# Score products of a head pair in one group per query tile, and a scheduler that counts changes of TensorE's array mode

## The chip, the cores and the metric

The program runs on one NeuronCore of a Trainium2 chip. The metric is device time in microseconds of one execution. The kernel before has a median of 554.98 us over three runs (554.88 to 555.44).

The core has five instruction streams that run beside each other and wait for each other through semaphores: TensorE (PE; its weight loads are listed apart as PEld), VectorE (DVE), ScalarE (ACT), GpSimd (POOL) and the DMA queue's engine (SP). Each takes its instructions in the order of the program.

## What is computed

One decoder layer over 1024 tokens of width 1024, in float32. `h` is the normalised input, scaled and shifted by a projection of the conditioning vector. One projection of `h` gives everything else:

```python
u_pool, g_pool, q, k, v, g_attn, qi, ki, wi = split(h @ w_in)
pool_out = pool_mixer(u_pool) * silu(g_pool)
# for each block of 128 queries:
score = sum_heads(relu(qi . ki) * wi)          # 8 index heads of 64, all 1024 keys
sel   = top_k(score, 256)                      # causal
p     = softmax(q . k[sel] / 8);  o = p @ v    # 8 heads of 64, 2 key heads
y     = concat(pool_out, o * silu(g_attn)) @ w_out
x     = x + gate * y
```

The selection is done by threshold: the kernel finds each query's 256th score by bisection over its bits, and adds a mask of zero or -1e30 to all scores in place of gathering keys.

## The kernel before, in words

Products are made from split operands: a float32 operand is cut into a rounded part and a rest (`hhi`, `hlo`; `wh`, `wl`), and three matmuls stand for one. Such a matmul is 128x128 by 128x512. The two kinds of score products (`ki` by `qi`, and `k` by `q`) are plain float32 with a contraction of 64. A pair of heads lies in the two halves of the 128 partitions, so the products of a pair use the upper and the lower 64 rows of the array. The products of probabilities with `v` are 64 columns wide, two side by side. So TensorE works in three array modes: all of the array, row halves, column halves. In the order of the program a float32 product is one instruction; in the trace it is two.

The text of the kernel does not fix the order of the work. It is written as generators ("strands"): each yields its next instruction (`Op`), a group of instructions that are to stand together (`Group`), a choice between engines (`Either`), a place in a pool (`Place`) or a condition. A planner, `Flow.run`, holds a clock for each engine with its own estimates of durations, and always issues the request with the least value of `wait`, to which it adds the strand's rank: `s[1]` (a number from `EARLY`, chosen by the kind under which the strand was spawned), or for a TensorE request `LAST` of that kind. So a change of the numbers `EARLY`, `LAST`, `SAFE`, `HOP` or `FAVOUR` moves instructions on all engines. `Op.wait` of a TensorE operation adds `safe`, which makes the planner issue it later than its data.

The parts that the prediction speaks of:

- `main_line`: the projection of `h` (`m<-hhi,wh` and its kind, fills TensorE from about 23 us to 329 us), in an order of tiles written in `ORDER`: `a` gates, `q` queries, `m` the pooling mixer (`u` and `gp`, then `mix`: `u` by a small matrix, `gp`, and its split `mph`, `mpl`).
- `index_scores`: for query tile 7 down to 2 and four head pairs, the products `m<-kiT,qix`; `score_relus` takes them out of PSUM on ACT (`kt`), and `score_sums` adds them up on DVE (`score`). PSUM has eight banks, and a place in it can be refused while fewer than `keep` are free (`IK`, `QK`).
- `selection`: the bisection, for tiles 5, 6, 7 on ACT (`ajunk`, then the small `aq`, `xq`), for tiles 2, 3, 4 on DVE (`junk`, `aq`, `xq`). 15 bits, then 16 bits. Between them and at the end DVE works on the masks (`selw`, `key`).
- `unit(i)`, i = 0 to 7: attention of a query tile. Products `m<-kT,qr`; `maxima` on DVE adds the mask and takes the maximum (`ex`, `mx`; it empties the bank); `exps` on ACT; `turns` transposes on TensorE (`m<-c,ex`), copied out as `pw`; `products` (`m<-pw,vrow`); `gated` (`mah`, `mal`). Unit i may start when unit i-1-FLY has ended.
- `output_line`: `project_pooled` (`m<-mph,wh`), then the first and the second half of `project_attended` (`m<-mah,wh`), 96 matmuls each for the halves. The second half needs all eight units and is the last work of the program.

Of the kernel before, what the change touches and what calls it, by code (L numbers as in the profile page):

```python
# [24 lines left out]
MASK_NEG = -1.0e30  # L25
KVW = 328

ORDER = "a2 a0 a1 q0 q1 | q2 m1 q3 m3 m2 m0 a3"
SWAP16 = [(i + 16) % 32 for i in range(32)]
WARM = [()] * 8  # L30
GROUPS = (((5, 6, 7), True), ((2, 3, 4), False))
# [4 lines left out]
ROOM = {"b": 36, "ld": 2, "st": 3, "wh": 4, "wl": 4, "kt": 2, "sg": 2, "selw": 1, "m": 8}  # L36


EARLY = {"main": 0.6, "fill": 0.4, "weights": 0.0, "evac": -1.0, "side": 0.2, "h": -0.2, "mods": -0.2, "select": -0.1,
         "scores": -0.6, "attend": -1.1, "late": 1.0, "kv": -0.3, "qi": -0.8, "pick": -0.6}  # L40

SELECT = -0.6
LAST = {"main": 0.12, "fill": 0.08}

SAFE = {"side": 1.0}

SCALED = (0,)

SUMS = (0,2,4,)

WKM = 6


HOP = 0.13
PHOP = 0
STT = 0.06
HOPS = {"PE": 0.19, "DVE": 0.13, ("ACT", "DVE"): 0.14, ("ACT", "ACT"): 0.035}

AGE = 0.37

PW_POOL = 0.4
XO_POOL = 0.38
BACK = 0.5
SPAN = 0.5

QK = 3
IK = 4
FK = 2
PK = 0
# [1 line left out]
MIX = 4  # L71
KEEP = 6

FLY = 1

PV = 2

WA_AHEAD = 3
AHEAD = 3
XN_AHEAD = 2  # L80

FAVOUR = {"DVE": 0.12, "ACT": -0.13, "POOL": 0.05}
TABLES = {AF.Silu: 1, AF.Sqrt: 2, AF.Exp: 3}


# [6 lines left out]
class Op:  # L92


    def __init__(self, eng, name, fn, args, kw):
        self.eng, self.name, self.fn, self.args, self.kw = eng, name, fn, args, kw
        aps = [a for a in args if isinstance(a, bass.AP)]
        named = [a for k, a in kw.items() if isinstance(a, bass.AP)]
        self.outs, self.ins = [], []
        for a in aps[:1] + [kw[k] for k in ("accum_out",) if kw.get(k) is not None]:  # L100
            self.outs.append(store(a))
            if a.free_size() == 1:
                self.outs.append((store(a), a.offset))
        for a in aps[1:] + named:
            self.ins.append((store(a), a.offset) if a.free_size() == 1 else store(a))
        self.us, self.safe = self._cost(aps, kw), 0.0
        self.shared = self._shared(aps)

# [12 lines left out]
    def _cost(self, aps, kw):  # L121
        size = [a.free_size() for a in aps]
        n = max(size)
        eng = self.eng
        if eng == "SP":
            return 0.42
        if eng == "PE":
            rate = 2 if self.name == "transpose" else 4 if aps[1].dtype == F32 else 1
            if rate == 4 and min(aps[0].shape[0], aps[1].shape[0]) == 64:
                rate = 2  # L130
            return max(0.109, size[0] * 0.000417 * rate + 0.0135)
        wide = [a for a, k in zip(aps, size) if k == n]
        psum = any(a.space == PSUM for a in wide)
        half = all(mybir.dt.size(a.dtype) == 2 for a in wide)
        if eng == "ACT":
            t = 0.000833 * n + (0.05 if psum else 0.094)
            t += 0.093 * sum(isinstance(kw.get(k), bass.AP) for k in ("scale", "bias", "accum_out"))
            return t
        if eng == "POOL":
            if self.name == "tensor_tensor":  # L140
                return 0.0021 * n + 0.147
            return 0.000833 * n + 0.16
# [28 lines left out]

    def issue(self, flow):
        t = self.start(flow)
        us = self.us
        if self.shared:
            flow.port = (t + us, self.eng)
        if self.eng == "ACT":
# [78 lines left out]
class Flow:  # L256
# [2 lines left out]

    def __init__(self):  # L260
        self.clock = dict.fromkeys(("PE", "DVE", "ACT", "POOL", "SP"), 0.0)
        self.dma, self.table = 0.0, None
        self.port, self.landed = (0.0, None), []
        self.ready, self.used, self.left, self.tag = {}, {}, {}, {}
        self.room = {k: [0.0] * n for k, n in ROOM.items()}
        self.strands = []
# [45 lines left out]
                req.issue(self)  # L312

    def spawn(self, gen, kind="side"):
        s = [gen, EARLY[kind], None, kind]
        self.strands.append(s)
        self.forward(s, None)

# [5 lines left out]
    def forward(self, s, val):  # L324
        try:
            s[2] = s[0].send(val)
            for o in s[2].ops if isinstance(s[2], Group) else [s[2]]:
                if isinstance(o, Op) and o.eng == "PE":
                    o.safe = SAFE.get(s[3], 0.0)
        except StopIteration:  # L330
            self.strands.remove(s)

# [28 lines left out]
def hybrid_layer(ctx, tc, xT, cT, nwT, badaT, wada, wq, wet, wkv, qnw, knw, wpool,  # L361
# [4 lines left out]
    flow = Flow()  # L366
# [526 lines left out]
    def index_scores():  # L893
        yield lambda: bool(ki)
        for i in (7, 6, 5, 4, 3, 2):
# [6 lines left out]
            for e in range(NH // 2):  # L902
                yield lambda: e in qi
                both = [], []
                for t, got in enumerate(both):
                    relus.append((i, 2 * e + t, got))
                for c0 in range(0, n, 512):
                    c1 = min(n, c0 + 512)
                    ops, put = [], []
                    for t in range(2):  # L910
                        ps = yield bank(keep=IK - 1 if t else IK)
                        r = slice(t * 64, t * 64 + 64)
                        ops.append(mm(ps[:, :c1 - c0], qi[e][r, i * P - 256:(i + 1) * P - 256],
                                      ki["T"][r, c0:c1], True, True))
                        put.append((c0, c1, ps))
                    yield Group(ops)
                    for t in range(2):
                        both[t].append(put[t])
        flow.drop(ki["T"], *[qi[e] for e in range(NH // 2)])

    parts = []
# [272 lines left out]
    def unit(i):  # L1194
# [42 lines left out]
        for e in range(4):  # L1237
            both = [], []
            for t in range(2):
# [2 lines left out]
                o = len(ex) % per * n  # L1242
                ex.append(slots[-1][:, o:o + n])
                flow.spawn(maxima(2 * e + t, both[t]), "attend")
            for c0 in range(0, n, 512):
                c1 = min(n, c0 + 512)
                ops, put = [], []
                for t in range(2):
                    ps = yield bank(keep=QK - 1 if t else QK)
# [3 lines left out]
                yield Group(ops)  # L1253
                for t in range(2):
                    both[t].append(put[t])
        if i == NT - 1:
            flow.drop(kT[0], *qT.values())

# [248 lines left out]
```

## Time and profile before

| | |
|---|---|
| median of the runs | 554.98 us |
| the profiled execution | 553.77 us |
| its span, first to last instruction | 552.1 us |
| PE busy | 516.8 us, 94% |
| DVE, ACT, POOL busy | 423.7, 372.5, 168.5 us |
| chain that ended last | PE 57%, DVE 27%, ACT 7%, issue 5% |

The profile shows one execution. A busy PE is not a PE at its best: its matmuls overlap, and how fast they follow each other is read from their starts in the timeline. PEclk is the granted clock as a share of 2.4 GHz. The stages overlap; by TensorE's work they are: start (to 103 us), index products between projections (103 to 172), projections while the selection runs (to 338), pooled output between attention units 0 to 4 (338 to 435), units 5 to 7 with the first half of the attended output (435 to 526), second half (to 552).

### The profile page before, as it was taken

What the parts mean: (1) busy time and instruction counts of PE and PEld (TensorE: products, weight loads), DVE (VectorE), ACT (ScalarE), POOL (GpSimd) and SP (SyncE); (2) the same over time, 40 slices, a digit from 0 to 9 for tenths busy, and PEclk for the clock granted to TensorE, in tenths of its full rate; (3) what the DMA queues carried; (4) which work ended last, traced back from release to release, by engine and by line L of the source; (5) the groups of instructions that cost most, each with busy time, mean ns of one, the idle gap of its engine ahead of it and who ended that gap; (6) DMA issues with size and microseconds to landing.
All of it is one profiled execution on the core that took longest, in us unless ns stands there. A gap on an engine that the chain in (4) does not pass through costs nothing.

```text
span 552.1 us, 7620 instructions
## 1 busy us (share of the span) xinstructions
PE 516.8 (94%) x2492; PEld 377.9 (68%) x2492; DVE 423.7 (77%) x895; ACT 372.5 (67%) x841; POOL 168.5 (31%) x179
## 2 busy tenths in 40 slices
PE   6969999999999999999997995999998999897997
PEld 6758899655657778868875863766676556545675
DVE  0699896787788999999999997985757996357142
ACT  6456721676478998998935988989896457818420
POOL 1399290221100246532434452420212242012000
PEclk9989999999999999999998997999999999998999
DMA  8994518010210111111110131634435222004044
GB/s 306 406 405 126 175 45 292 28 58 19 77 59 0 39 39 57 58 39 39 39 38 20 39 114 60 207 96 155 134 126 176 81 79 95 1 19 150 23 150 155
DMA packets 28023, 58.29 MB, mean 106 GB/s; under 512 B 3792, under 2 KB 7888, under 8 KB 27984
## 3 DMA queue, kind: packets, MB, share of 16 engines
q1 hardware_dynamic: 27984, 57.81, 30.5%
q8 instruction: 19, 0.31, 0.2%
q14 instruction: 20, 0.16, 0.1%
HBM read 47.32 MB, written 10.49 MB: 105 GB/s over the span
## 4 chain that ended last, share of the span: by engine, by line
PE 57%; DVE 27%; ACT 7%; issue 5%; DMA 2%; POOL 1%; SPq 0%; DVEq 0%; POOLq 0%; ACTq 0%
PE m L182 57%; DVE junk L182 9%; ACT ex L182 4%; DVE selw L182 3%; DVE ex L182 3%; DMA xt<-xT 2%; DVE sw L182 1%; DVE xq L182 1%; DVE mx L182 1%; ACT ajunk L182 1%; DVE wa L182 1%; DVE nx L182 1%; DVE aq L182 1%; DVE key L182 1%; DVE hlo L182 1%
## 5 line engine op out<-in xcount | busy, mean ns | idle before, releaser
L182 PE MATMUL m<-hhi,wh 128*128 128x512 f32 (+1 forms) x320 | 121.6, 402 | 1.0 <-ACT hhi L182 1.0
L182 PE MATMUL m<-hlo,wh 128*128 128x512 f32 (+1 forms) x320 | 115.2, 385 | 4.5 <-DVE hlo L182 4.5
L182 PE MATMUL m<-hhi,wl 128*128 128x512 f32 (+1 forms) x320 | 115.4, 382 | 0.0
L182 ACT ACTIVATE ajunk<-key,xq 128x768 bf16<-128x768 uint16 (+2 forms) x93 | 96.5, 1038 | 5.8 <-DVE xq L182 4.6
L182 PEld LDWEIGHTS m<-hhi,wh 128*128 128x128 f32 x320 | 59.5, 191 | 25.8 <-issue 12.4
L182 DVE TENSOR_SCALAR_CACHE_REDUCE junk<-key,xq 128x384 bf16<-128x384 uint16 (+2 forms) x93 | 69.3, 745 | 2.8
L182 PEld LDWEIGHTS m<-hlo,wh 128*128 128x128 f32 x320 | 59.2, 190 | 17.0 <-DVE hlo L182 5.3
L182 POOL TENSOR_TENSOR wl<-ld,wh 128x512 fp32r<-128x512 f32 x42 | 63.3, 1512 | 20.3 <-ACT wh L182 11.3
L182 ACT ACTIVATE ex<-ex,mx,c 128x256 f32<-128x256 f32 (+6 forms) x64 | 54.8, 858 | 19.4 <-DVE mx L182 13.3
L182 PEld LDWEIGHTS m<-hhi,wl 128*128 128x128 f32 x320 | 59.4, 190 | 12.3 <-issue 1.7
L182 POOL TENSOR_SCALAR wh<-ld 128x512 fp32r<-128x512 f32 x28 | 19.6, 698 | 108.3 <-PE m L182 96.1
L182 DVE SCALAR_TENSOR_TENSOR score<-kt,c,score 128x1024 f32<-128x1024 f32 (+5 forms) x42 | 42.9, 1022 | 11.3 <-ACT kt L182 9.4
L182 ACT ACTIVATE kt<-m 128x512 f32<-128x512 f32 (+1 forms) x80 | 37.9, 527 | 13.8 <-DVE score L182 8.6
L182 PE MATMUL m<-c,ex 128*128 128x128 f32 x288 | 37.8, 284 | 7.3 <-ACT ex L182 7.1
L182 PEld LDWEIGHTS m<-c,ex 128*128 128x128 f32 x288 | 33.8, 147 | 11.2 <-ACT ex L182 9.2
L182 PE MATMUL m<-kT,qr 64*128 64x512 f32 (+3 forms) x192 | 39.6, 511 | 1.6 <-DVE mx L182 1.6
L182 DVE SCALAR_TENSOR_TENSOR xo<-m,c,xo 128x512 f32<-128x512 f32 x24 | 17.9, 748 | 28.4 <-PE m L182 27.0
L182 DVE CUSTOM_DVE_ANT_0 ex<-m,key 128x512 f32<-128x512 f32 (+1 forms) x48 | 30.5, 663 | 7.8 <-PE m L182 7.8
L182 PE MATMUL m<-kiT,qix 64*128 64x512 f32 (+3 forms) x160 | 34.1, 542 | 0.0
L182 PEld LDWEIGHTS m<-kT,qr 64*128 64x128 f32 x192 | 18.7, 186 | 21.8 <-issue 13.7
L182 PE MATMUL m<-pw,vrow 128*64 128x512 f32 x144 | 33.3, 600 | 0.0
L182 PE MATMUL m<-mph,wh 128*128 128x512 f32 x64 | 26.4, 413 | 4.5 <-DVE mph L182 4.5
(186 smaller groups left out, 1017.4 us busy)
## 6 DMA issues: line engine op xcount, KB each, us to landing
wa<-wada SPq DMA_DIRECT2D x24, 512.0 KB, 7.5
ld<-wet SPq DMA_DIRECT2D x16, 512.0 KB, 3.3
ld<-wout SPq DMA_DIRECT2D x24, 256.0 KB, 2.9
xo<-xT SPq DMA_DIRECT2D x16, 256.0 KB, 3.2
y_d<-xo SPq DMA_DIRECT2D x16, 256.0 KB, 2.3
xo<-y_d SPq DMA_DIRECT2D x16, 256.0 KB, 2.9
outT<-xo SPq DMA_DIRECT2D x16, 256.0 KB, 2.1
xt<-xT SPq DMA_DIRECT2D x7, 512.0 KB, 7.7
```

The source lines that it names most:

```text
L182: self.fn(*self.args, **self.kw)
```

## The change

The products of a head pair are collected over all keys of the query tile and yielded as one `Group` (two or four products), for the index scores and for attention; before, each stretch of 512 keys was a group of two. The first place of a group is asked for with `keep` `IK` (`QK`), each further one with one less.

The planner knows array modes: an operation with a contraction of 64 is "rows", one with 64 output partitions "columns", any other "all"; when the mode changes, the planner's TensorE clock is moved by `SWITCH` of the mode that is left. Strands are ranked by the name of their generator where `EARLY` (and `SAFE`) has it, else by their kind as before. Many of the planner's numbers are others. Attention may run two units ahead (`FLY` 2), and two loads may start earlier (`WKM`, `WA_AHEAD`).

```diff
-ORDER = "a2 a0 a1 q0 q1 | q2 m1 q3 m3 m2 m0 a3"
+ORDER = "a2 a0 a1 q1 q2 | q0 m1 q3 m3 m2 m0 a3"
 EARLY: the old entries, and 24 new ones by generator, as
+         "mix": -0.36, "rotated": -0.18, "query_loads": 0.01, "exps": -0.11, "score_sums": -1.13,
-SELECT = -0.6
-LAST = {"main": 0.12, "fill": 0.08}
+SELECT = -0.461
+LAST = {"main": 0.12, "fill": 0.129, "scores": 0.008}
-SAFE = {"side": 1.0}
+SAFE = {"side": 1.0, "unit": 0.1, "query_norms": 0.67, "rotated": 0.7, "norm": 0.45, "weight_loads": 0.1}
-WKM = 6
+WKM = 4
+SWITCH = {"all": 0.1, "rows": 0.25, "columns": 0.32}
-QK = 3
+QK = 4
-FLY = 1
+FLY = 2
-WA_AHEAD = 3
+WA_AHEAD = 5
...
     def issue(self, flow):
         t = self.start(flow)
+        if self.eng == "PE" and self.mode != flow.mode:
+            t = max(t, flow.clock["PE"] + SWITCH[flow.mode])
...
     def spawn(self, gen, kind="side"):
-        s = [gen, EARLY[kind], None, kind]
+        s = [gen, EARLY.get(gen.__name__, EARLY[kind]), None, kind]
...
+                ops, put = [], []
                 for c0 in range(0, n, 512):
                     c1 = min(n, c0 + 512)
-                    ops, put = [], []
                     for t in range(2):
-                        ps = yield bank(keep=IK - 1 if t else IK)
+                        ps = yield bank(keep=max(IK - len(ops), 0))
                         r = slice(t * 64, t * 64 + 64)
                         ops.append(mm(ps[:, :c1 - c0], qi[e][r, i * P - 256:(i + 1) * P - 256],
                                       ki["T"][r, c0:c1], True, True))
                         put.append((c0, c1, ps))
-                    yield Group(ops)
-                    for t in range(2):
-                        both[t].append(put[t])
+                yield Group(ops)
+                for n2, p in enumerate(put):
+                    both[n2 % 2].append(p)
```

The same edit stands in `unit` for `kT` and `QK`. `SELECT` is the rank of the ACT selection after all index scores are summed. Three places show what became of the order.

TensorE in the index stage, the fourth head pair of query tile 7 (`kiT`: index keys, `qix`: index queries), before:

```order
L182 MATMUL m<-hlo_457,wh_697 128x512
L182 MATMUL m<-kiT_943,qix_632 128x512 x2
L182 MATMUL m<-hhi_512,wh_697 128x512
L182 MATMUL m<-hhi_512,wl_698 128x512
L182 MATMUL m<-hlo_513,wh_697 128x512
L182 MATMUL m<-hhi_557,wh_697 128x512
L182 MATMUL m<-hhi_557,wl_698 128x512
L182 MATMUL m<-hlo_558,wh_697 128x512
L182 MATMUL m<-kiT_943,qix_632 128x512 x2
```

and the same pair now, followed by the first pair of tile 6:

```order
L196 MATMUL m<-hlo_457,wh_705 128x512
L196 MATMUL m<-kiT_942,qix_633 128x512 x4
L196 MATMUL m<-kiT_942,qix_607 128x512 x2
L196 MATMUL m<-kiT_942,qix_607 128x384 x2
L196 MATMUL m<-hhi_512,wh_705 128x512
L196 MATMUL m<-hhi_512,wl_706 128x512
L196 MATMUL m<-hlo_513,wh_705 128x512
```

The two stretches of keys that six projection matmuls parted now stand together, and the next pair follows without a projection between.

DVE at the last step of the pooling mixer (`gp`; `junk`, `aq`, `xq`: bits of the DVE selection; `ex`, `mx`: maxima of attention units 0 and 1), before:

```order
L182 TENSOR_SCALAR junk_3213,cq_726_3185<-key_85,xq_713_3157 128x640
L182 ISA ex_3221,mx_2543<-m,mask_82 128x256
L182 ISA mx_2543 128x1
L182 ISA ex_3172,mx_2541<-m,mask_82 128x128
L182 ISA mx_2541 128x1
...
L182 SCALAR_TENSOR_TENSOR gp_2753<-m,c_97,gp_2753 128x512
L182 TENSOR_TENSOR aq_739_3241<-cq_726_3185,kcq_245_1503 128x3
L182 SCALAR_TENSOR_TENSOR mx_2543<-mx_2543,c_102 128x4
L182 SCALAR_TENSOR_TENSOR tlq_279_1638<-aq_739_3241,yq_740_3242 128x3
```

and now:

```order
L196 TENSOR_SCALAR junk_3091,cq_684_3090<-key_83,xq_679_3076 128x384
L196 SCALAR_TENSOR_TENSOR gp_2746<-m,c_97,gp_2746 128x512
L196 TENSOR_SCALAR junk_3093,cq_684_3090<-key_84,xq_679_3076 128x512
L196 SCALAR_TENSOR_TENSOR gp_2746<-m,c_97,gp_2746 128x512
L196 TENSOR_SCALAR junk_3099,cq_684_3090<-key_85,xq_679_3076 128x640
L196 TENSOR_TENSOR aq_693_3114<-cq_684_3090,kcq_244_1469 128x3
L196 SCALAR_TENSOR_TENSOR xq_694_3115<-aq_693_3114,yq_695_3116 128x3
```

Before, the last `gp` stood behind every bit of the DVE selection (`tlq` is its result) and behind all 16 maxima of units 0 and 1. Now the last bits, with 10 `junk` counts in all, and the 16 maxima stand behind it.

TensorE in the tail, the score products of unit 7 (`kT` by `qr`, 512 wide and without a rest) and the products of unit 6 (`pw` by `vrow`), before:

```order
L182 MATMUL m<-pw_4598,vrow_633 64x512 x2
L182 MATMUL m<-pw_4609,vrow_633 64x512 x2
L182 MATMUL m<-kT_1505,qr_1357 128x512 x4
L182 MATMUL m<-kT_1505,qr_1530 128x512 x4
L182 MATMUL m<-kT_1505,qr_1665 128x512 x2
L182 MATMUL m<-mah_3498,wh_4145 128x512
L182 MATMUL m<-mah_3498,wl_4146 128x512
L182 MATMUL m<-mal_3499,wh_4145 128x512
```

and now, where these `pw` are still those of unit 5:

```order
L196 MATMUL m<-pw_4486,vrow_634 64x512 x2
L196 MATMUL m<-pw_4514,vrow_634 64x512 x2
L196 MATMUL m<-kT_1465,qr_1564 128x512 x4
L196 MATMUL m<-pw_4533,vrow_634 64x512 x2
L196 MATMUL m<-pw_4546,vrow_634 64x512 x2
L196 MATMUL m<-kT_1465,qr_2086 128x512 x4
L196 MATMUL m<-pw_4557,vrow_634 64x512 x2
L196 MATMUL m<-pw_4570,vrow_634 64x512 x2
L196 MATMUL m<-c_76,ex_4280 128x128
```

Unit 7's scores moved from behind unit 6's last product to between unit 5's products, ahead of unit 6's transposes (`m<-c,ex`). Behind unit 6's last product unit 7's transposes now follow at once.

## Rows read from the trace of the kernel before

**Rows 1.** The page: the span, and part 1, busy time of each engine.

```profile
span 552.1 us, 7620 instructions
PE 516.8 (94%) x2492; PEld 377.9 (68%) x2492; DVE 423.7 (77%) x895; ACT 372.5 (67%) x841; POOL 168.5 (31%) x179
```

**Rows 2.** Busy time by stretch: length; PE, PEld, DVE, ACT, POOL (instructions); PEclk, DMA.

```profile
103.30:176.00 72.70, 72.70 (x318) 41.49 (x318) 56.78 (x72) 50.83 (x103) 11.85 (x13) 1.00 0.13 44
240.00:338.30 98.30, 87.37 (x378) 67.24 (x377) 94.97 (x247) 74.64 (x182) 41.72 (x50) 0.97 0.17 54
338.30:435.20 96.90, 94.98 (x482) 65.87 (x482) 69.56 (x167) 82.54 (x218) 19.37 (x23) 0.98 0.43 139
435.20:490.00 54.80, 51.93 (x278) 30.10 (x278) 34.83 (x95) 30.36 (x60) 12.13 (x10) 1.00 0.15 49
490.00:526.00 36.00, 31.04 (x158) 20.05 (x154) 19.25 (x45) 19.83 (x37) 5.12 (x5) 0.91 0.21 66
```

**Rows 3.** What PE waited for, 103 to 552 us: total us, times, longest.

```profile
PE m L182 <- ACT ex L182: 7.1, 5, 2.1
PE m L182 <- DVE mph L182: 4.5, 1, 4.5
PE m L182 <- DVE u L182: 4.0, 1, 4.0
PE m L182 <- DVE mx L182: 1.6, 1, 1.6
```

**Rows 4.** PE's timeline in the index stage: start, us, instruction.

```profile
103.02 0.40 PE L182 MATMUL m<-hlo,wh 128*128 128x512 f32 x1
103.34 1.99 PE L182 MATMUL m<-kiT,qix 64*128 64x512 f32 x8
105.26 0.50 PE L182 MATMUL m<-hhi,wh 128*128 128x512 f32 x1
105.60 0.39 PE L182 MATMUL m<-hhi,wl 128*128 128x512 f32 x1
105.83 0.40 PE L182 MATMUL m<-hlo,wh 128*128 128x512 f32 x1
...
106.86 3.70 PE L182 MATMUL m<-kiT,qix 64*128 64x512 f32 x16
110.49 0.51 PE L182 MATMUL m<-hhi,wh 128*128 128x512 f32 x1
```

**Rows 5.** Busy time by stretch, directly behind three of PE's waits.

```profile
293.20:298.00 4.80, 4.72 (x12) 3.46 (x13) 4.73 (x13) 3.35 (x7) 0.23 (x1) 0.64 0.00 0
338.20:344.00 5.80, 5.74 (x16) 4.22 (x17) 2.07 (x3) 5.78 (x19) 0.00 (x0) 0.64 0.01 3
507.70:514.00 6.30, 6.16 (x32) 5.77 (x33) 2.27 (x4) 4.11 (x8) 0.00 (x0) 0.58 0.57 192
```

**Rows 6.** Groups: counts of the DVE selection, maxima of units 0, 1, an ACT cast.

```profile
L182 DVE TENSOR_SCALAR_CACHE_REDUCE junk<-key,xq 128x384 bf16<-128x384 uint16 (+2 forms) x93 | 69.3, 745 | 2.8
...
L182 DVE CUSTOM_DVE_ANT_0 ex<-m,mask 128x256 f32<-128x256 f32 x8 | 3.2, 414 | 0.0
L182 DVE CUSTOM_DVE_ANT_0 ex<-m,mask 128x128 f32<-128x128 f32 x8 | 2.1, 284 | 0.1
...
L182 ACT CAST wh<-ld 128x512 fp32r<-128x512 f32 x25 | 15.2, 617 | 9.2 <-PE m L182 9.2
```

**Rows 7.** The timeline, 420 to 510 us: points of PE, the mask of tile 5 (DVE).

```profile
422.65 0.33 PE L182 MATMUL m<-c,ex 128*128 128x128 f32 x1 [1.49 <-ACT ex L182]
...
429.03 0.36 DVE L182 TENSOR_SCALAR key<-selw 128x768 bf16<-128x768 bf16 x1
...
435.15 2.42 PE L182 MATMUL m<-kT,qr 64*128 64x512 f32 x12
...
488.76 4.66 PE L182 MATMUL m<-kT,qr 64*128 64x512 f32 x20
...
507.73 3.40 PE L182 MATMUL m<-c,ex 128*128 128x128 f32 x13 [2.12 <-ACT ex L182]
```

More of the change, by code (lines that the diff above doesn't have):

```diff
@@ L36 @@
 ROOM = {"b": 36, "ld": 2, "st": 3, "wh": 4, "wl": 4, "kt": 2, "sg": 2, "selw": 1, "m": 8}
-EARLY = {"main": 0.6, "fill": 0.4, "weights": 0.0, "evac": -1.0, "side": 0.2, "h": -0.2, "mods": -0.2, "select": -0.1,
-         "scores": -0.6, "attend": -1.1, "late": 1.0, "kv": -0.3, "qi": -0.8, "pick": -0.6}
-SELECT = -0.6
-LAST = {"main": 0.12, "fill": 0.08}
-SAFE = {"side": 1.0}
+EARLY = {"main": 0.6, "fill": 0.4, "weights": 0.0, "evac": -1.0, "side": 0.2, "h": -0.2, "mods": -0.2,
+         "select": -0.1, "scores": -0.6, "attend": -1.1, "late": 1.0, "kv": -0.3, "qi": -0.8, "pick": -0.6,
+         "mix": -0.36, "rotated": -0.18, "query_loads": 0.01, "exps": -0.11, "score_sums": -1.13,
+         "key_value_out": -0.58, "index_queries": -1.39, "norm": -2.29, "gate_loads": -0.03, "token_scales": -0.31,
+         "gate_mods": 0.58, "unit": -0.41, "index_scores": -0.39, "lead_loads": 1.53, "out": -1.53, "lead_out": -0.72,
+         "weight_loads": -0.1, "key_value_weights": -0.24, "main_line": 1.04, "output_line": 0.3, "turns": -1.82,
+         "finish": -0.62, "index_keys": -0.9, "h_block": -0.1, "attention_keys": -0.68, "turned": -1.72,
+         "h_blocks": -0.05, "gated": -1.24}
+SELECT = -0.461
+LAST = {"main": 0.12, "fill": 0.129, "scores": 0.008}
+SAFE = {"side": 1.0, "unit": 0.1, "query_norms": 0.67, "rotated": 0.7, "norm": 0.45, "weight_loads": 0.1}
 SCALED = (0,)
 SUMS = (0,2,4,)
-WKM = 6
-HOP = 0.13
-PHOP = 0
-STT = 0.06
+WKM = 4
+HOP = 0.103
+PHOP = -0.008
+STT = 0.062
 HOPS = {"PE": 0.19, "DVE": 0.13, ("ACT", "DVE"): 0.14, ("ACT", "ACT"): 0.035}
+SWITCH = {"all": 0.1, "rows": 0.25, "columns": 0.32}
 AGE = 0.37
 PW_POOL = 0.4
-XO_POOL = 0.38
+XO_POOL = 0.45
 BACK = 0.5
 SPAN = 0.5
-QK = 3
+QK = 4
 IK = 4
@@ L72 @@
 KEEP = 6
-FLY = 1
+FLY = 2
 PV = 2
-WA_AHEAD = 3
+WA_AHEAD = 5
 AHEAD = 3
 XN_AHEAD = 2
-FAVOUR = {"DVE": 0.12, "ACT": -0.13, "POOL": 0.05}
+FAVOUR = {"DVE": 0.122, "ACT": -0.13, "POOL": 0.013}
 TABLES = {AF.Silu: 1, AF.Sqrt: 2, AF.Exp: 3}
@@ L105, in __init__ @@
             self.ins.append((store(a), a.offset) if a.free_size() == 1 else store(a))
+        self.mode = "all"
         self.us, self.safe = self._cost(aps, kw), 0.0
@@ L129, in _cost @@
             if rate == 4 and min(aps[0].shape[0], aps[1].shape[0]) == 64:
+                self.mode = "rows" if aps[1].shape[0] == 64 else "columns"
                 rate = 2
@@ L176, in issue @@
             flow.port = (t + us, self.eng)
+        if self.eng == "PE":
+            flow.mode = self.mode
         if self.eng == "ACT":
@@ L261, in __init__ @@
         self.clock = dict.fromkeys(("PE", "DVE", "ACT", "POOL", "SP"), 0.0)
-        self.dma, self.table = 0.0, None
+        self.dma, self.table, self.mode = 0.0, None, "all"
         self.port, self.landed = (0.0, None), []
@@ L328, in forward @@
                 if isinstance(o, Op) and o.eng == "PE":
-                    o.safe = SAFE.get(s[3], 0.0)
+                    o.safe = SAFE.get(s[0].__name__, SAFE.get(s[3], 0.0))
         except StopIteration:
@@ L1244, in unit @@
                 flow.spawn(maxima(2 * e + t, both[t]), "attend")
+            ops, put = [], []
             for c0 in range(0, n, 512):
                 c1 = min(n, c0 + 512)
-                ops, put = [], []
                 for t in range(2):
-                    ps = yield bank(keep=QK - 1 if t else QK)
+                    ps = yield bank(keep=max(QK - len(ops), 0))
                     r = slice(t * 64, t * 64 + 64)
@@ L1252, in unit @@
                     put.append((c0, c1, ps))
-                yield Group(ops)
-                for t in range(2):
-                    both[t].append(put[t])
+            yield Group(ops)
+            for n2, p in enumerate(put):
+                both[n2 % 2].append(p)
         if i == NT - 1:
```

## The prediction, made before the changed kernel was run

> **What bounds the kernel now.** I read the page first: PE is busy 516.8 of 552.1 us [rows 1], so only 35.3 us of the span are PE's idle time, and a faster kernel needs less PE time or fewer waits. Then the table by stretches [rows 2], to see who else is full where: in the index stage PE is busy without a gap, DVE 56.8 and ACT 50.8 of 72.7 us; from 240 to 338 us DVE is (94.97 of 98.3 us) and PE is not (87.4); from 338 to 435 us PE again (94.98 of 96.9); in the tail no engine is full, PE comes first (51.9 of 54.8 and 31.0 of 36.0). Then PE's waits [rows 3]: 4.5, 4.0 and 1.6 us on DVE lie in the middle, and 7.1 us in five waits on ACT's exponentials, one of them (1.5 us, in front of unit 4's transposes [rows 7]) before 435 us and four in the tail. Last the timelines at the places that the order moves. So three things can be won: changes of array mode where PE is full, DVE's lateness in the middle, and the latency of one attention unit in the tail.
>
> **Changes of mode.** What a visit to the row mode costs is read from the index stage [rows 4]. Eight rows of 512 columns (two groups) take 105.26 - 103.34 = 1.92 us from start to start, sixteen (four groups) 110.49 - 106.86 = 3.63, so a group more costs (3.63 - 1.92) / 2 = 0.855 us. From the last ordinary matmul before (103.02) to the second one after (105.60) it is 2.58 us; two groups are 1.71 and two ordinary steps (105.60 to 105.83) 2 x 0.23 = 0.46; 0.41 us are left for going in and out. I counted the visits in both orders: index products come in 13 visits in place of 21, attention's scores in 19 in place of 20, the products with `v` in 12 in place of 11. The last two cancel; 8 x 0.41 = 3.3 us go. Between the first and the last index product stand 102 projection matmuls in place of 132, so PE could be through with the index scores 3.3 + 30 x 0.23 = 10 us earlier; only the 3.3 are saved, the 30 come later. Bounds: 3.7 us if the column visit costs nothing, 0 if PE waits for banks instead.
>
> That wait has to be priced. DVE's 56.8 us of work stay (1 to 2 more by my count), and the stage would shrink from 72.7 to about 62.5 us: DVE would be over 90% full, ACT over 80% [rows 2]. A group of four now holds four banks of eight at once. I put 3 us of PE waits here. The Trainium skill (page "TensorEngine Tiling (Array Packing)", section Performance Considerations) warns that tiling the array speeds TensorE up but not the emptying of PSUM, which may become the bottleneck. The trace before agrees only halfway, since PE had no wait here while the two engines that empty the banks had 22% and 30% to spare; by the rule alone the whole of this term would be lost, and what it would do to the rest is the first rival.
>
> **The middle.** The waits on DVE up to 338.3 us are 4.5 + 4.0 + 1.6 = 10.1 us [rows 3]. Behind two of them PE ran at a mean granted clock of 0.64, a mix of 1.2 and 2.4 GHz: (1 - 0.64) x 4.8 = 1.7 and 0.36 x 5.8 = 2.1 us [rows 5]. Together 13.9 us. All of it hangs on DVE being full. In the new order 10 counts of the DVE selection and the 16 maxima of units 0 and 1 stand behind the last `gp` where all stood ahead: 10 x (0.745 + 0.08) + 8 x 0.414 + 8 x 0.284 + 16 x 0.08 = 15.1 us [rows 6] (0.08 is a read of the accumulator, an estimate from the gaps between such pairs). Counted from the start, the other moves on DVE up to that point cancel, and it reaches `gp` with 15 us less to do; it also begins up to 10 us earlier. So the first pooled output, which started at 338.3 us when `mph` came, can start when PE is ready for it: 338.3 - 13.9 - 3.3 = 321 us. I keep back the 3 us of the index stage and 2.5 more for the last `mph`, which is cast on ACT and finished on POOL now, where a count of the ACT selection can stand in front: 326.6 us. What is late next is the masks of tiles 2 to 4, behind the moved counts; 108 pooled matmuls, 25 us, stand ahead of the first transposes and cover that. Bounds: 13.9, or nothing if DVE is late all the same.
>
> **338 to 435 us.** PE is full; 24 matmuls of the attended output's first half stand here now in place of the tail (5.4 us, moved and not saved); 36 of them in front of unit 4's transposes cover the 1.5 us wait there. I take 0 for the stretch (bounds -1.9, all of its idle time, to +3 for the later masks). Unit 5 would begin at 326.6 + (435.2 - 338.3) - 2.1 (slow clock gone, already counted) + 5.4 = 427 us in place of 435.2. It needs its mask from the ACT selection (429.0 before [rows 7]). ACT has 12 instructions more between its first and its last bit, mostly weight casts; at the 0.617 us of such a cast that is 7.4 us [rows 6], against an earlier start of 5 to 10. I take the mask as unmoved or a little earlier.
>
> **The tail.** Unit 7 may now start while units 5 and 6 run. Before, its scores began at 488.8 us, behind unit 6's last product, and its transposes waited twice for exponentials, up to 507.7 us [rows 7]. Now scores, maxima and exponentials lie beside unit 6's transposes, and unit 7's transposes follow unit 6's products at once. Removed: 7.1 - 1.5 = 5.6 us of waits [rows 3], and (1 - 0.58) x 6.3 = 2.6 us of slow clock behind the last one [rows 5], 8.2 in all. But the maxima of units 6 and 7 share DVE, and those of unit 6 that are still open are now behind some of unit 7. I keep back 4.5 us for unit 5's and unit 6's transposes waiting longer: 3.7 us. Bounds: 8.2, or +2 (second rival). The last half and the wait in front of it stay.
>
> **The sum.** 552.1 - 3.3 - (13.9 - 5.5) - 3.7 = 536.7 us of span. Around the span lie 553.77 - 552.1 = 1.7 us, and the median of the runs is 1.2 us above the profiled execution: 539.6, so 540 us.
>
> **Rivals.**
>
> *The banks bind the index stage* (0.15). For it: DVE over 90%, four banks at once. Against: PE had no wait there, and ACT and DVE together had 38 us to spare. Then the 3.3 us go to waits, the selection starts no earlier, the 30 projections pushed behind still have to be done before 338, and I leave 5 of the middle's 13.9: 552.1 - 5 - 3.7 = 543.4, 546 us.
>
> *DVE binds the tail* (0.13). For it: DVE's work from 435 to 526 us is 34.8 + 19.3 = 54.1 us [rows 2], and in the new order all of it but unit 7's last maxima and copies, some 47, stands ahead of unit 6's transposes. Full from the mask on, 429 + 6 + 47 and 5 for the exponentials, it would free them at 487 us; before, unit 6 was through with its products at 488.8 [rows 7]. Against: DVE was idle 36% of 435 to 490 us [rows 2], and the mask may come earlier. Then the tail gives +2 in place of -3.7: 542.4, 545 us.
>
> *Only the mode changes count* (0.08), the rest of the moves being neutral: 552.1 - 3.3 = 548.8, 552 us. For it: orders that a planner likes need not suit the chip. Against: the 15 us on DVE are a count and no estimate of the planner.
>
> *Slower: the ACT selection comes late* (0.11). Each cast put between its bits can wait for its load or for a free buffer, and all later bits wait behind it on ACT, then masks, maxima, exponentials and TensorE. From the mask of tile 5 to the end it is 552.1 - 429.0 = 123.1 us; less 5.4 (moved ahead) and 3.7 it is 114.0. So from a mask at 438 us, 9 us later than now, the kernel is slower: the 7.4 us of casts without an earlier start, and a few waits of the kind that stood before such casts (9.2 us in all [rows 6]), would do it. At 443 us it is 557 of span, 560 us. Against: the index scores end earlier, and ACT has 14.4 us without work from 338 to 435 [rows 2].
>
> **How the numbers follow.** 0.53 for the forecast, whose own range is 533 to 546. A difference under 0.2% (1.1 us) is no change in a measurement of this kernel. The third rival lies at the edge: I count 0.02 of it, and 0.03 of the slower one, as the same. Faster 0.86, same 0.05, slower 0.09. Range 529 to 553: below lies only the sum with nothing kept back (552.1 - 3.3 - 13.9 - 8.2 + 2.9 = 529.6) and a little luck, above it most of the slower case.
>
> **What would show it.** Right: the index products end near 160 to 165 us in place of 172; PE's waits on `u` and `mph` shrink to under 4 us, and `mph` products start near 327; `kT` products of unit 5 near 427; no PE wait of over 1 us between unit 6's products and unit 7's transposes; no low clock behind 490 us. Wrong: waits of the index products on `kt` or `score` (first rival); ACT exponentials as the releaser of long waits at unit 5's and 6's transposes (second); tile 5's mask later than 438 us (slower). The forecast is wrong as a whole if the pooled output still starts near 338 us.

## The result and the profile after

The changed kernel takes 532.5 us in the median of four runs (529.42 to 535.14), the kernel before 555.2 beside it: a ratio of 0.958 (95% interval 0.952 to 0.964). A second set of five (experiment 9) gave 529.8 us and 0.955 (0.952 to 0.957). The forecast was 540 us in 529 to 553: the direction was right and the gain was forecast too small. As the stages show, one term came as worked out, the middle gave less than its terms in this profile, and the tail much more.

The page of the changed kernel, its profiled execution being the slowest of the four (535.14 us):

```profile
span 533.2 us, 7630 instructions
PE 510.2 (96%) x2492; PEld 378.2 (71%) x2492; DVE 427.3 (80%) x895; ACT 376.4 (71%) x848; POOL 160.5 (30%) x173
```

Against [rows 1] PE's idle time fell from 35.3 to 23.0 us; its busy time fell by 6.6 us, with the same instructions. The stretches that answer to [rows 2], cut where the stages now end (columns as there):

```profile
104.00:162.00 58.00, 58.00 (x267) 34.07 (x267) 49.62 (x64) 45.44 (x94) 2.38 (x5) 1.00 0.11 37
240.00:332.50 92.50, 86.06 (x370) 66.67 (x368) 88.14 (x208) 68.79 (x164) 44.31 (x52) 0.95 0.16 50
332.50:432.50 100.00, 100.00 (x505) 70.23 (x504) 78.61 (x195) 91.47 (x242) 29.56 (x31) 0.98 0.47 149
432.50:490.00 57.50, 56.45 (x306) 33.35 (x306) 48.94 (x137) 37.65 (x68) 8.55 (x8) 1.00 0.22 67
490.00:507.20 17.20, 15.98 (x108) 9.83 (x104) 4.11 (x6) 7.97 (x18) 0.73 (x1) 1.00 0.00 1
```

In the index stage DVE rose to 86% and ACT to 78%, and PE still has no gap. In the middle DVE is 95% busy (97% before) and PE 93% (89%), with the clock low for a while. From 332.5 us on PE is full but for 2.3 us. What PE waited for, 103 to 533 us (total, times, longest), against [rows 3]:

```profile
PE m L196 <- DVE mx L196: 3.5, 2, 1.8
PE m L196 <- DVE u L196: 2.8, 1, 2.8
PE m L196 <- ACT mah L196: 1.3, 1, 1.3
PE m L196 <- ACT ex L196: 0.8, 2, 0.5
```

The wait on `mph` is gone, two waits on maxima have come, and the exponentials cost 0.8 us in place of 7.1. The points of the timeline that answer to [rows 7], PE (first index product, the instruction behind the last one, then as there), the mask of tile 5 and the last `gp`:

```profile
103.96 5.42 PE L196 MATMUL m<-kiT,qix 64*128 64x512 f32 x24
161.05 0.50 PE L196 MATMUL m<-hhi,wh 128*128 128x512 f32 x1
321.34 0.75 DVE L196 SCALAR_TENSOR_TENSOR gp<-m,c,gp 128x512 f32<-128x512 f32 x1
332.57 0.79 PE L196 MATMUL m<-mph,wh 128*128 128x512 f32 x1
422.58 0.71 DVE L196 TENSOR_SCALAR key<-selw 128x768 bf16<-128x768 bf16 x1
432.55 2.85 PE L196 MATMUL m<-kT,qr 64*128 64x512 f32 x16
491.81 7.15 PE L196 MATMUL m<-c,ex 128*128 128x128 f32 x64
507.23 0.50 PE L196 MATMUL m<-mah,wh 128*128 128x512 f32 x1 [1.26 <-ACT mah L196]
```

All 64 transposes of unit 7 run without a wait. In the kernel before, the instruction behind the last index product and the last `gp` were

```profile
170.38 0.50 PE L182 MATMUL m<-hhi,wh 128*128 128x512 f32 x1
335.77 0.74 DVE L182 SCALAR_TENSOR_TENSOR gp<-m,c,gp 128x512 f32<-128x512 f32 x1
```

By stages:

| start, us | before | after | after, profile of experiment 9 | forecast |
|---|---|---|---|---|
| index products | 103.3 | 104.0 | 102.5 | |
| pooled output | 338.3 | 332.6 | 327.3 | 326.6 |
| scores of unit 5 | 435.2 | 432.6 | 426.8 | 427 |
| second half | 526.1 | 507.2 | 501.5 | 510.7 |
| end | 552.1 | 533.2 | 527.5 | 536.7 |

(The forecast of the second half is its span less the 26.0 us that remain.)

### The profile page after: what moved, and what is told of

It is laid out like the page before. It is cut to its first block, busy times and chain, and to the rows that moved or that the text cites. A ratio compares the mean times of both kernels' runs of the same rounds, so it can differ in the third digit from the quotient of the medians.

```text
span 533.2 us, 7630 instructions
## 1 busy us (share of the span) xinstructions
PE 510.2 (96%) x2492; PEld 378.2 (71%) x2492; DVE 427.3 (80%) x895; ACT 376.4 (71%) x848; POOL 160.5 (30%) x173
## 4 chain that ended last, share of the span: by engine, by line
PE 55%; DVE 31%; ACT 6%; issue 5%; DMA 1%; POOL 1%; SPq 0%; DVEq 0%; POOLq 0%
PE m L196 55%; DVE junk L196 9%; ACT ex L196 4%; DVE ex L196 3%; DVE selw L196 3%; DVE aq L196 2%; DVE nx L196 1%; DVE sw L196 1%; DVE xq L196 1%; DVE key L196 1%; DVE wa L196 1%; DVE u L196 1%; DVE hlo L196 1%; DVE qr L196 1%; DVE gp L196 1%
## 5 line engine op out<-in xcount | busy, mean ns | idle before, releaser
L196 POOL TENSOR_TENSOR wl<-ld,wh 128x512 fp32r<-128x512 f32 x40 | 61.6, 1542 | 33.8 <-ACT wh L196 15.3
L196 ACT ACTIVATE ex<-ex,mx,c 128x256 f32<-128x256 f32 (+7 forms) x64 | 54.8, 858 | 2.2 <-DVE mx L196 2.1
L196 DVE SCALAR_TENSOR_TENSOR score<-kt,c,score 128x1024 f32<-128x1024 f32 (+5 forms) x42 | 39.9, 950 | 6.7 <-ACT kt L196 4.8
L196 PEld LDWEIGHTS m<-c,ex 128*128 128x128 f32 x288 | 31.7, 140 | 5.9 <-ACT ex L196 2.8
L196 PE MATMUL m<-c,ex 128*128 128x128 f32 x288 | 35.1, 275 | 0.8 <-ACT ex L196 0.8
L196 PE MATMUL m<-kiT,qix 64*128 64x512 f32 (+3 forms) x160 | 32.2, 532 | 0.0
L196 POOL TENSOR_SCALAR_AFFINE_SELECT score<-score 128x128 f32<-128x128 f32 x6 | 3.1, 510 | 91.1 <-PE m L196 46.5
L196 ACT CAST wh<-ld 128x512 fp32r<-128x512 f32 x35 | 21.4, 617 | 11.2 <-PE m L196 11.2
```

## The experiments

**1 and 2. Unit 7 alone, put in and taken out.** The first is the kernel before with

```diff
-            yield lambda: i in masks and len(ended) >= i - FLY
+            yield lambda: i in masks and len(ended) >= i - FLY - (i == NT - 1)
```

and one more buffer for its maxima; the second the changed kernel with `+ (i == NT - 1)`. Up to unit 7 the order of each is that of its origin.

> The kernel before, with one edit: unit 7 may start when unit 4 has ended, the others as before (the order up to that point is unchanged). Theory A (the tail was bound by the latency of unit 7 alone: scores behind unit 6's last product, then maxima and exponentials with too little work beside them): the waits of transposes on exponentials behind unit 5 (5.6 us) and the slow clock after the last (2.6 us) go, 8 us, about 547 us. The changed kernel's stretch from unit 5's scores to the second half was 74.7 us against 90.9, 5.5 of it moved ahead; if all the rest came from this edit it would be 10.8 us, 544 us. Rival B (unit 7's maxima take DVE from units 5 and 6, their transposes wait longer): 553 to 557 us. Rival C (the tail gained from the earlier mask and the matmuls moved ahead): 554 to 556 us.

> The changed kernel, with one edit: unit 7 may start only when unit 5 has ended, as before the change; the order up to there is that of the changed kernel. Theory A: its scores stand behind unit 6's products again, and no first-half matmul is left to fill the time, so the 19 us from unit 7's scores to its last exponential (488.8 to 507.7 in the kernel before) are covered only by its scores (4.7) and by transposes that can go: 8 to 14 us more, 541 to 547 us, with waits on ACT's exponentials and a low clock behind them. Rival B or C (the tail gained otherwise): 531 to 536 us.

Measured: 550.8 us, ratio 0.991 (0.989 to 0.993), and 550.4 us, 0.992 (0.989 to 0.994). So unit 7's early start is worth 4.9 us in the old order and 18 to 21 in the new one (against 532.5 and 529.8 us): a result between theory A and B, then one beyond A. The tail of the second (PE):

```profile
482.33 8.02 PE L196 MATMUL m<-kT,qr 64*128 64x512 f32 x32
496.73 0.47 PE L196 MATMUL m<-c,ex 128*128 128x128 f32 x1 [6.38 <-ACT ex L196]
499.18 0.47 PE L196 MATMUL m<-c,ex 128*128 128x128 f32 x1 [1.97 <-ACT ex L196]
```

Nothing is left to stand between unit 7's scores and its transposes, and the granted clock is 0.51 for 14 us (third number from the end):

```profile
494.00:508.00 14.00, 5.23 (x21) 3.96 (x22) 2.74 (x9) 11.48 (x19) 0.00 (x0) 0.51 0.00 0
```

In the first, 6.4 us of waits on exponentials stay (7.1 before), now in front of units 4 to 7, while 30 first-half matmuls stand behind unit 7's last product. Why the planner left them there was not tested.

**3 and 4. The groups of the index stage alone, put in and taken out.** The hunk of `index_scores` in the diff is applied to the kernel before, or undone in the changed one.

> The kernel before, with the index products of a head pair in one group per query tile and the asked-for spare banks falling by one for each product; attention's groups, the planner's numbers and its blindness to modes stay. 17 visits to the row mode in the index stage in place of 21. Theory A (0.41 us a visit): the stage, first to last index product, loses 4 x 0.41 = 1.6 us besides the projections that change sides; the run is 1 to 2 us faster, 553.5 us. Rival (a group of four waits for banks): no gain, PE waits on kt or score in the stage, 555 to 557 us.

> The changed kernel with the index products in groups of two as before; everything else stays, also the accounting of modes. 17 visits in the index stage in place of 13; the pooling mixer's last products stand 2 counts of the DVE selection later. Theory A: 1.6 us more for the visits, 1 to 4 us with the later mixer: 534 to 537 us. Rival (the merge is the change, the rest of the planner's numbers follow from it): back by half or more, 540 us and above.

Measured: 558.0 us, ratio 1.004 (1.003 to 1.006), and 556.4 us, 1.001 (0.999 to 1.003). The index stage of the third did what was expected; both totals lie above theory A. From the first index product to the instruction behind the last, less 0.2275 us for each projection in between:

| kernel | visits | stage, us | projections | left |
|---|---|---|---|---|
| before | 21 | 67.04 | 132 | 37.01 |
| 3, before with groups | 17 | 65.44 | 132 | 35.41 |
| 8, changed, planner blind | 17 | 62.63 | 120 | 35.33 |
| 4, changed without groups | 17 | 58.16 | 96 | 36.32 |
| changed | 13 | 57.09 | 102 | 33.89 |

0.39 to 0.40 us a visit (1.60 / 4 and 3.12 / 8). The fourth kernel lies 0.9 above the others with 17 visits, and its trace says where: 0.75 us of it in one visit. Its 5632 columns would take 2.6 us at the pace of [rows 4] (0.855 us for 2048 columns, and 0.21 for the visit); they took 3.3. Its last products began as ACT ended three readings of PSUM, at 119.2 to 120.1 us, with a table load in front of these:

```profile
117.85 3.39 PE L196 MATMUL m<-kiT,qix 64*128 64x512 f32 x12
117.30 1.28 ACT L196 ACT_TABLE_LOAD   x1
```

That is a wait for banks which the profile does not list as idle time. The changed kernel has one too, 0.26 us, in its second visit.

But the third is 2 us slower in all. Its waits on DVE (PE, 103 us to the end):

```profile
PE m L182 <- DVE u L182: 7.0, 2, 4.0
PE m L182 <- DVE mph L182: 3.5, 1, 3.5
PE m L182 <- DVE mx L182: 1.7, 1, 1.7
PE m L182 <- DVE qsl L182: 1.6, 1, 1.6
```

The planner laid the middle anew, and it came out with 13.8 us of such waits in place of 10.1 [rows 3]: the 1.6 us were given back. The fourth lost most of its gain behind 333 us (195.7 us to the second half, against 174.7), in waits on exponentials, with 30 first-half matmuls left over behind unit 7:

```profile
PE m L196 <- ACT ex L196: 14.0, 8, 4.6
```

Its total is what the rival said, but for another reason: put into the kernel before, the groups gained nothing, so what the fourth lost came with another tail that the planner laid.

**5 and 6. The mixer alone, and three edits together.** Five is the kernel before with this, six the kernel before with the edits of 1, 3 and 5 together.

```diff
-        flow.spawn(mix(), "side")
+        flow.spawn(mix(), "pool")
-         ... "pick": -0.6}
+         ... "pick": -0.6, "pool": -0.9}
-SAFE = {"side": 1.0}
+SAFE = {"side": 1.0, "pool": 1.0}
```

> The kernel before, with the last steps of the pooling mixer ranked ahead of the DVE selection (-0.9 in place of 0.2, the selection has -0.6). The last gp stands behind 79 of the selection's 93 counts in place of 93. Theory A (the middle is bound by DVE's order): 14 x 0.825 us, 11.5 us less in front of it; the pooled output starts at 329 to 333 us in place of 338.3 and PE's waits on u and mph fall from 8.5 us to under 4. In the tail this order spends the first-half matmuls earlier and puts all 16 score products of unit 7 with nothing behind unit 6's products; by what the second experiment showed that gives back 6 to 14 us: 550 to 558 us in all. Rival B (the middle is bound by PE or ACT): the pooled output starts at 336 us or later. Rival C (what is won in the middle reaches the end): 547 us or less.

> The kernel before, with three edits and none of the table of numbers: the index products in one group per query tile (as in the third experiment), the mixer's rank (as in the fifth), and unit 7 free to start when unit 4 has ended (as in the first). In its order unit 7's scores stand between unit 6's transposes and products, and no first-half matmul is left behind unit 7's. Theory A (three local things make the gain): index stage 65.4 us, pooled output at 329 to 334 us, tail without waits of over 1.5 us: 534 to 542 us. Rival (the table of numbers makes it, by many small moves): 545 to 552 us.

Measured: 556.5 us, ratio 1.003 (1.001 to 1.005), and 548.3 us, 0.988 (0.986 to 0.990). Five did in its place what was expected: pooled output at 332.9 us in place of 338.3, waits on `u` 1.1 us and none on `mph`, though 5.3 us on maxima. The tail gave all of it back, as theory A had allowed (PE's waits on exponentials, 103 us to the end):

```profile
PE m L182 <- ACT ex L182: 11.8, 7, 3.3
```

Its mask of tile 5 came at 440.4 us, 11.4 later than before. Six has a tail with few waits (1.6 us on exponentials), but in its middle 7.2 us of waits on `u` and 3.6 on maxima. Its time is the rival's. The 15.8 us between it and the changed kernel lie in what it left out: the table of numbers, but also the accounting of modes, attention's groups, `ORDER` and `FLY` for the other units. Of these only the accounting was tested alone (experiment 8).

**7. The changed kernel with the mixer ranked higher.**

```diff
-         "mix": -0.36,
+         "mix": -0.9,
```

> The changed kernel with the mixer's rank at -0.9 in place of -0.36: the last gp behind 77 of 93 counts of the DVE selection in place of 83, the last small product of u 8 to 9 counts earlier. Theory A (the 2.8 us wait on u, the two waits on maxima of 3.5 us and the low clock behind them, 3.9 and 3.4 us by the profile, come from DVE's order): u's wait goes with its low clock, 526 to 531 us. Rival (the time moves to the maxima of units 0 and 1, or the masks of tiles 2 to 4 come too late behind the counts that are pushed back): 532 to 538 us.

Measured: 542.9 us, ratio 0.978 (0.974 to 0.981): slower than the changed kernel by 10 us or more, outside both ranges, although the pooled output starts at 323.6 us, earlier than in any other. No wait on `u` is left; in its place stands one of 4.4 us on maxima. Behind the start (PE, 323.7 us to the end) there are

```profile
PE m L196 <- ACT st L196: 4.1, 3, 2.0
PE m L196 <- ACT ex L196: 2.3, 2, 1.7
PE m L196 <- ACT mah L196: 1.3, 1, 1.3
PE m L196 <- DVE mah L196: 1.1, 1, 1.1
PE m L196 <- POOL st L196: 1.1, 1, 1.1
```

and from there to the second half it takes 192.7 us, against 174.7 (after) and 187.8 (before).

**8. The changed kernel with a planner blind to modes.**

```diff
-SWITCH = {"all": 0.1, "rows": 0.25, "columns": 0.32}
+SWITCH = {"all": 0.0, "rows": 0.0, "columns": 0.0}
```

> The changed kernel with all three entries of SWITCH at zero, so that the planner counts no changes of mode; the groups stay. 17 visits to the row mode in the index stage in place of 13, 36 in all in place of 32; the tail keeps unit 7's scores between unit 6's transposes and leaves no first-half matmul behind. Theory A (a visit costs 0.41 us, the order of the tail makes the rest): 4 x 0.41 = 1.6 us more, 532 to 536 us. Rival (every edit of the planner loses the order that was found, as in the fourth experiment): 545 us and above.

Measured: 542.9 us, ratio 0.978 (0.976 to 0.981), between the two theories. Of the visits saved in the index stage half come from the groups (21 to 17) and half from the accounting (17 to 13); the rest of the 10.4 us lies in the middle (2.9 us more up to the pooled output) and behind it (180.1 us to the second half in place of 174.7, with 4.9 us of waits).

**9 to 12. The order held fast.** The planner's choice was written out as a list of turns that the next kernels follow, so that a move changes only what it names:

```diff
-            s = min(ready, key=lambda s: s[2].wait(self) + (LAST.get(s[3], 0.0) if s[2].eng == "PE" else s[1]))
+        for n, entry in enumerate(PLAN.split()):
+            uid, pick = entry.split(".")
```

Nine is the changed kernel again. Ten moves the two small products of `u` at 300 us on PE (and with them the `gp` that takes them up on DVE); eleven does that, moves the last counts of the DVE selection behind the maxima and swaps two `mpl` on POOL; twelve has neither move, but two bits less, so its result is not the layer's:

```diff
-m<-u,c
 six projections
-m<-u,c
 six projections
+m<-u,c
 six projections
+m<-u,c
...
-            for b in range(nbits - 1, -1, -1):
+            for b in range(nbits - 1 if act or nbits == 15 else 13, -1, -1):
```

> The changed kernel once more, as the measure for the two beside it: 529 to 535 us.

> The changed kernel with its order written out and kept in every engine, and one move: the two small products of u at about 300 us stand two groups of six projections (2.7 us) later on PE, so that u is there when PE comes to them. Theory A (the wait of 2.8 us and the low clock behind it, 3.4 us by the windows of 2 us, are on the path, all that follows moves ahead): u's wait goes, 526 to 531 us, and less spread over the runs. Rival (the masks of the ACT selection and the maxima on DVE set the time of the attention units, PE only waits later): no change, 530 to 535 us.

> The same with a second move: the three counts of the DVE selection, aq and xq that stand ahead of and among the maxima of units 0 and 1 stand behind them, and on POOL the rest mpl that is wanted first is made first. The waits on maxima (1.7 and 1.8 us) and the low clock behind them (3.4 us) go too, the pooled output starts at 320 to 323 us in place of 332.6. Theory A (PE is the path up to the end): 6.3 us of waits and 6.8 us of low clock, 13 us less at most, 519 to 524 us. Theory B (the masks of tiles 5 to 7, at 422.6, 428.9 and 441.1 us, come from ACT and do not move; unit 5's scores would then stand 3 us ahead of their mask, and the transposes of units 5 to 7 wait): 524 to 530 us. Rival (the masks of tiles 2 to 4, 5 us later on DVE, hold up units 2 to 4): 532 us or more.

> The changed kernel with its order written out and kept, and two of the 31 bits of the DVE selection left out (the first two of the second 16; the thresholds of tiles 2 to 4 are then coarse): 6 counts, 2 aq and 2 xq fewer on DVE, 6 x 0.825 + 4 x 0.16 = 5.6 us, between 265 and 275 us; ACT's selection is untouched. Theory A (DVE's load binds the middle, so that two moves of order only shifted the wait): the waits on u and on maxima (1.9 and 3.1 us in the last run of the changed kernel) and the low clock behind them (3.9 us) go, the pooled output starts at 318 to 321 us in place of 327.3, and the run takes 521 to 524 us. Theory B (the same, but the masks of tiles 5 to 7 come from ACT and stay, so the tail gives a part back): the pooled output starts at 318 to 321 us, 524 to 527 us. Rival (PE's work or ACT bind the middle): 529 us or more.

Measured, in the order 9 to 12: 529.8, 531.7, 531.2 and 526.8 us; ratios 0.955 (0.952 to 0.957), 0.958 (0.955 to 0.961), 0.956 (0.953 to 0.959) and 0.949 (0.947 to 0.952). In the tenth the wait at 300 us is gone and comes back at the next small product:

```profile
299.71 1.02 PE L394 MATMUL m<-u,c 128*128 128x512 f32 x2
314.44 1.98 PE L394 MATMUL m<-u,c 128*128 128x512 f32 x4 [1.90 <-DVE u L394]
```

So its time is the rival's. The eleventh has no gain either, and lies between theory B and its rival: the first wait on maxima went, the second is 2.4 us, behind a `mpl` that took 2.65 us on DVE, and `u` waits 2.5 us at 314.8. Only the twelfth, which takes work from DVE, has no wait on `u`, and starts the pooled output 222.3 us behind the first index product in place of 224.8. Its time is theory B's, its place is not: the pooled output started at 326.2 us, where both theories had 318 to 321, so 5.6 us less work on DVE became 2.5.

```profile
326.23 0.79 PE L394 MATMUL m<-mph,wh 128*128 128x512 f32 x1
322.40 0.93 DVE L394 TENSOR_TENSOR aq<-cq,kcq 128x3 f32<-128x3 f32 x1
```

Its two waits on maxima are still there (1.7 and 1.8 us). The first ends behind three counts that stand ahead of the maxima; it went in the eleventh, where they were moved. The second ends behind an `aq` and a `mpl` that stand among the maxima (the `aq` above took 0.93 us; the last section says why that is long). So the wait on `u` went with DVE's load, and those on maxima with DVE's order. PE in all four is full from there to the second half (174.2 to 175.4 us). Theory B of the eleventh has no support: the mask of tile 5 came 89.5 to 90.8 us behind the start of the pooled output in all of 9 to 12, so it moved with it, over the 3 us that this start moved. None of the complete kernels beats the changed one.

What the twelve say together (us; PE's waits behind the start of the pooled output; the kernel before took 555.1 to 555.9 us beside each set):

| kernel | index to pooled | pooled to second half | waits in it | median |
|---|---|---|---|---|
| before | 234.9 | 187.8 | 8.2 | 555.2 |
| 1 | 234.9 | 183.9 | 6.8 | 550.8 |
| 3 | 239.3 | 187.5 | 8.3 | 558.0 |
| 5 | 228.7 | 198.4 | 12.7 | 556.5 |
| 6 | 236.0 | 180.0 | 3.5 | 548.3 |
| changed | 228.6 | 174.7 | 1.0 | 532.5 |
| 9, changed | 224.8 | 174.2 | 1.1 | 529.8 |
| 10 | 225.1 | 174.8 | 1.1 | 531.7 |
| 11 | 225.5 | 175.4 | 1.9 | 531.2 |
| 12, two bits less | 222.3 | 174.5 | 1.1 | 526.8 |
| 2 | 224.8 | 194.3 | 16.0 | 550.4 |
| 4 | 230.3 | 195.7 | 14.5 | 556.4 |
| 7 | 221.1 | 192.7 | 10.1 | 542.9 |
| 8 | 231.5 | 180.1 | 4.9 | 542.9 |

In kernels 1 to 8 and before, each microsecond of waits behind the pooled output goes with 1.3 to 2.1 us more of this stretch than in the changed kernel. That is a comparison of orders, and not a test of the waits alone.

## Why the forecast was right, and where it was not

**Changes of mode: right.** 3.3 us were forecast, 37.01 - 33.89 = 3.1 measured; the index products ended at 161.1 us, inside 160 to 165. The first rival, banks, came only as the 0.26 us found under experiments 3 and 4: the profile lists no wait of PE in the stage, at 86% of DVE and 78% of ACT. The Trainium skill's warning on emptying PSUM (page "TensorEngine Tiling (Array Packing)", section Performance Considerations) is hardly borne out at these loads.

**The marks of the forecast.** The 2.1 us of low clock behind 338.2 us lie after the start of the pooled output. The forecast took them off ahead of that start and once more behind it; its sum of 536.7 us has them once. By the terms of the sum the pooled output belonged at 328.7 us and unit 5's scores at 428.9, in place of 326.6 and 427.

**The middle: right in direction, too large in one profile.** From the first index product to the pooled output it went from 234.9 to 228.6 us in the first profile, 6.3 us less, and 10.1 less in the second; by the terms of the sum 9.6 were forecast. DVE was ahead as counted: the last `gp` began 14.4 us earlier, where 15.1 us less work was the count. But "less to do up to `gp`" did not clear the way for `u` and for the maxima, which stand elsewhere in DVE's row. A wait on `u` stayed (2.8 us), maxima took `mph`'s place (3.5), and behind both the clock was low:

```profile
298.00:308.00 10.00, 8.02 (x19) 5.07 (x20) 8.13 (x22) 6.25 (x16) 0.79 (x4) 0.66 0.08 26
330.00:338.00 8.00, 6.79 (x19) 5.05 (x20) 7.75 (x35) 4.90 (x14) 2.17 (x2) 0.58 0.39 121
```

(1 - 0.66) x 10 and (1 - 0.58) x 8, 3.4 us each, where I had counted that loss as gone. The 5.5 us kept back covered this in the second profile and not in the first, which is luck. A cost on DVE that the count did not have is in the last section.

**338 to 435 us: the number right by luck.** 100.2 us were forecast from pooled output to unit 5's scores (96.9 - 2.1 + 5.4), 100.0 and 99.5 measured. But the low clock behind the start did not go: the granted clock of the whole stretch is 0.98 before [rows 2] and after, 2 us of loss in each. What went in its place are the 1.9 us of PE's idle time, which the forecast had left standing. The mask of tile 5 was taken as unmoved; it came 6.4 us earlier in the first profile.

**The tail: right in its cause, mis-sized, and this is where the forecast fell short.** From unit 5's scores to the second half 90.9 us became 74.7 in both profiles, 16.2 less. 5.5 of it moved ahead; 10.7 are won where 3.7 were forecast, with a bound of 8.2. The term that was mis-sized is the 4.5 us kept back for units 5 and 6: their transposes hardly wait (the two on exponentials together 0.8 us). 5.3 us of waits and the 2.6 us of low clock went, as in the full term; the other 2.8 lie in shorter steps of transposes, scores and first-half matmuls, and were not tested. That keeping something back was no mistake in general shows in experiments 1, 2, 4, 5 and 7, where such waits stayed or grew.

So in the first profile a middle that gave 3.3 us less and a tail that gave 7 us more than forecast partly cancel; 540 us lies nearer to the result than its terms do.

**The slower rival** did not come here, but its mechanism is seen in experiment 5: ACT's last bit ended at 429.7 us in place of 416.2, the mask came at 440.4, and the kernel is slower by 0.3%, close to the point that I had worked out (438). It does not decide alone: experiment 6 has its mask at 443.7 us and is faster, with units 5 to 7 overlapped.

**The third rival** (only the modes count) falls, and so does its opposite: no single part put into the kernel before gained more than 4.9 us, and no edit of one part of the changed one that left the planner free lost less than 10. What is shown is that the gain behind the pooled output hangs on unit 7's early start (experiment 2, the same order up to there) together with an order in which transposes hardly wait. Which of the planner's numbers make that order stays open; attention's groups, `ORDER` and the loads were never tested alone.

## What to carry to other kernels

A gain read off one stage can be exact there and still not reach the end: 1.6 us of modes and 5.4 us of DVE order were measured in place and given back later, because the planner laid the rest anew. Where a planner sets the order, hold the order fast before judging one part, and judge a whole order by what the bottleneck engine waits in its last third. And moving work in the row of a full engine moved the wait in experiments 7, 10 and 11; taking work from it removed one in experiment 12.

## What the runs showed that was not expected

One program, 5.7 us apart. The two profiles of the changed kernel run the same instructions. They part at 33 us (a wait on DVE's `hlo`) and at 300 us. PE in the first profile:

```profile
35.64 1.22 PE L196 MATMUL m<-hlo,wh 128*128 128x256 f32 x4 [2.81 <-DVE hlo L196]
299.98 2.08 PE L196 MATMUL m<-u,c 128*128 128x512 f32 x2 [2.78 <-DVE u L196]
```

and in the second, with the stretch behind its wait on `u`:

```profile
33.55 1.22 PE L196 MATMUL m<-hlo,wh 128*128 128x256 f32 x4 [0.60 <-DVE hlo L196]
297.59 1.12 PE L196 MATMUL m<-u,c 128*128 128x512 f32 x2 [1.89 <-DVE u L196]
297.00:307.00 10.00, 9.41 (x38) 7.10 (x39) 9.36 (x28) 9.66 (x26) 4.70 (x7) 1.00 0.09 30
```

Behind 2.8 us of waiting the granted clock was 0.66 over ten us, behind 1.9 us it was 1.00: a wait 0.9 us longer, and the pooled output came another 2.9 us later. The length of the wait alone does not decide it. Behind a wait of 1.7 us on maxima at 322.1 us the second profile has a low clock too:

```profile
323.00:331.00 8.00, 6.59 (x22) 4.44 (x21) 7.86 (x37) 6.15 (x17) 3.90 (x3) 0.57 0.60 190
```

And two engines slowed each other. A `mpl` of 128x1024 on DVE, and two that POOL makes, in experiment 11:

```profile
324.94 2.65 DVE L395 TENSOR_TENSOR mpl<-gp,mph 128x1024 fp32r<-128x1024 f32 x1
324.15 5.65 POOL L395 TENSOR_TENSOR mpl<-gp,mph 128x1024 fp32r<-128x1024 f32 x2 [1.30 <-ACT mph L395]
```

In experiment 12 DVE's stood behind POOL's two, which ended at 323.3 us:

```profile
323.25 1.21 DVE L394 TENSOR_TENSOR mpl<-gp,mph 128x1024 fp32r<-128x1024 f32 x1
318.65 4.67 POOL L394 TENSOR_TENSOR mpl<-gp,mph 128x1024 fp32r<-128x1024 f32 x2
```

Side by side DVE's took 1.4 us longer and POOL's two 1.0. (Beside DVE's of 1.21 us stood a `wl` of POOL that began just after it and took 2.33 us, where others took 1.3: the one that began first was not slowed.) The same befalls DVE's smallest instructions, and it accounts for the 0.9 us above (other such meetings ahead of it about cancel). In the first profile an `xq` of three columns ahead of the late `u` began beside POOL's `wl` and ended with it, at 298.1 us:

```profile
297.01 1.12 DVE L196 SCALAR_TENSOR_TENSOR xq<-aq,yq 128x3 f32<-128x3 f32 x1
296.85 1.26 POOL L196 TENSOR_TENSOR wl<-ld,wh 128x512 fp32r<-128x512 f32 x1 [3.08 <-ACT wh L196]
298.71 1.22 DVE L196 SCALAR_TENSOR_TENSOR u<-nx,u 128x1024 f32<-128x1024 f32 x1
```

In the second profile DVE was past the same `xq` before `wl` began; it took 0.16 us, and `wl` 2.15 beside `u`:

```profile
295.58 0.16 DVE L196 SCALAR_TENSOR_TENSOR xq<-aq,yq 128x3 f32<-128x3 f32 x1
296.51 2.15 POOL L196 TENSOR_TENSOR wl<-ld,wh 128x512 fp32r<-128x512 f32 x1 [4.17 <-ACT wh L196]
```

Counted from the first index product, this `u` came 0.9 us later in the first profile. From 240 us to the pooled output the `aq` and `xq` took 4.2 us more than 0.16 each in the kernel before, 9.7 in the first profile after and 6.6 in the second. The count of DVE's work had no such term, and a busy DVE is partly a DVE that stands beside POOL. Whether an order that keeps POOL's `wl` away from them would free `u` was not tested.
